# A hybrid attention layer: the running sums of the forget gates and the first layer of the compressed branch at other places in TensorE's queue

## The chip, the cores and the metric

The kernel runs on one core of a Trainium2 chip, in one launch. The metric is the device time of a run in microseconds. A core has a matrix engine (TensorE, PE in the profile; its loads of stationary operands are PEld), a vector engine (VectorE, DVE), a scalar engine for activation functions (ScalarE, ACT), a general engine (GpSimd, POOL) and an engine that mostly starts transfers (SyncE, SP). Each works through a queue of its own in order and waits on semaphores for what the others have made. SBUF holds the tiles, PSUM the results of matmuls, HBM the weights.

## The reference, cut to what matters

Two layers on a sequence of 512 rows of 1024 numbers. Each layer is a feed-forward block, a block of token mixing and another feed-forward block, with a layer norm behind each. The token mixing projects the rows with one wide matrix into the queries, keys and values of three kinds of attention and some gates:

```
q_a, kv_a, g_a, q_b, k_b, v_b, q_c, k_c, v_c, f_c = _split_cols(h @ w_in)
o_a = _nsa(q_a, kv_a, g_a, ...)          # compressed + selected + window
o_b = _swa_sink(q_b, k_b, v_b, sinks, ...)  # window of 128, with a sink
o_c = _fox(q_c, k_c, v_c, f_c, b_f)      # forget gates
```

Two pieces of it are touched here. The forget gates enter as a running sum over the sequence:

```
log_f = jax.nn.log_sigmoid((f_c + b_f).astype(jnp.float32))
c = jnp.cumsum(log_f, axis=1)
logits = q @ k * scale + c[query] - c[key]
```

And the compressed branch of the first kind makes one key and one value out of each 32 rows, with a small two-layer network, `gelu(flat @ w1) @ w2`, where `flat` has 2048 numbers and the hidden layer has 256.

## The kernel before

All numbers are four bytes wide. Where a product has to be exact, an operand is split into a high and a low part, and three matmuls (high by high, low by high, high by low; L161, L162 and L163 in `mm3`) add up in PSUM. One slice `k` of a projection is thus three matmuls of 128 x 128 by 512 columns, and a projection of 128 output columns is eight such slices, called parts here.

The function `mix` is the token mixing. TensorE's and GpSimd's instructions run in exactly the order in which the code issues them (a manual schedule). Those of VectorE, ScalarE and SyncE are ordered by the tile framework, which also puts in the semaphores and hands out the buffers of a pool; tiles that share a tag share its buffers.

The order of TensorE's work is made by two things. A double-ended queue `fill` holds closures: `chunk` (L826) appends the eight parts of a projection, and the last part calls the evacuation of the result from PSUM. `pump(n)` (L891) pops and runs closures until n of them have counted; those wrapped by `free` (L809) don't count. A function `step` (L970) works on batches of attention units, `cur` and `prev`. It issues the scores of `cur` (`u.s()`) and the transposes of the probabilities of `prev` (`u.tr()`) in turn, with parts from `fill` between them, and ends with the value products of `prev` (`u.pv`, into the PSUM tile `po`). Ahead of a unit's scores it pumps until `need(u)` holds, that is, until its query and keys have been made. The list `PUMPS` (L1010) says how many closures go into each of the 21 steps. The first eight batches are pairs of units of the windowed attention (`Swa`), the later ones are units of the forget-gate attention (`Fox`) and of the first kind (`Nsa`).

The names that matter:

- `ev_q` (L398) takes a query from PSUM into the tile `qs`: a ScalarE copy (L403) and a VectorE subtraction (L404), twice, one behind the other. `set_q` (L841) lets it count as made four places further down in `fill`.
- `ev_gf` (L438) takes the gates from PSUM; its `rest` transposes them on TensorE (`gfT`, L445) and runs a chain of small VectorE and ScalarE instructions up to the logarithm of the forget gates (`f`, L465). Its `cum` (L471) makes the running sums with seven small matmuls a layer against a triangle of ones or ones alone (`cum`, L475 and L478; each matmul of this kind is two records, so 28 in two layers), and the result goes through HBM (`ncd`) to tiles `nck`. `set_gf` (L899) puts `late`, which calls `rest`, at place 4 of `fill` and `cum` at place 14 or the end.
- `ev_z` (L489) takes the compressed key's or value's projection from PSUM and adds position codes: eight VectorE additions (L500, L502) into two tiles `z`, which take buffers of the tag `p`. This tag has 14 buffers (`PB`) and mostly holds probabilities.
- `conv` (L506) is the first layer of the compressed branch. Before, it is eight closures `part(j)`. Each takes a buffer of the tag `raw` (three buffers, shared with all weights that stream in), loads two transfers of 256 KB into it and issues four matmuls with a 128 x 64 stationary operand and 256 columns (`hid`, L522, eight records). Keys go to rows 0 to 63 of the result and values to rows 64 to 127. Behind the last one comes the gelu. `tr` transposes the result (`glT`), and `conv2` (L547) is the second layer.
- `ps` hands out PSUM buffers by tag: two of `mm` for projections, three of `sc` for scores and for `hid`, two of `tp` for transposes, one of `po` for value products.

Before, the stage issues 29 closures ahead of the first step: the windowed attention's key, its first query, the gates, half of its second query and the gate transposes. The running sums follow behind the second half of that query. The compressed key, the third query and the compressed value come next, and then the eight parts of `conv` one by one between parts of the fourth query and the first `Fox` projections.

Of the kernel before, what the change touches and what calls it, by code (L numbers as in the profile page):

```python
# [9 lines left out]
F32 = mybir.dt.float32  # L10
# [8 lines left out]
P = 128  # L19
# [45 lines left out]
def body(tc, a, out, depth=DEPTH):  # L65
    nc = tc.nc
# [46 lines left out]
    def wraw(shape=None):  # L113
        return wt.tile(list(shape or [P, KD, P]), F32, name="raw", tag="raw", bufs=3)
# [237 lines left out]
    def mix(l, wts, pend, done_ffn, xap, xa, nxt):  # L352
        m = K()
        PB = 14
# [151 lines left out]
        def conv(ws):  # L506


            c = K()
            wv = [w.rearrange("(c p) f -> p c f", p=P) for w in ws]  # L510

            def part(j):
                def go():
                    if j == 0:
                        c.p = ps("sc", "hid", (P, 256))
                    r = wraw([P, 2, 2, 256])
                    for i in range(2):
                        nc.sync.dma_start(r[:, i], wv[i][:, 2 * j:2 * j + 2])
                    for k in (2 * j, 2 * j + 1):
                        for i in range(2):  # L520
                            z = (m.zk, m.zv)[i][k // 8][:, k % 8].rearrange("p g n -> p (g n)")
                            nc.tensor.matmul(c.p[64 * i:64 * i + 64], z, r[:, i, k % 2], start=k == 0, stop=k == 15)  # L522
                    if j == 7:
                        x = at.tile([P, 2, 256], F32, name="gl", tag="p", bufs=PB)
                        t, c.t = x[:, 0], x[:, 1]
                        nc.scalar.activation(t, c.p, AF.Square)
                        nc.vector.tensor_scalar(t, t, 0.044715, 1.0, op0=OP.mult, op1=OP.add)
                        nc.vector.tensor_tensor(t, t, c.p, op=OP.mult)
                        nc.scalar.activation(t, t, AF.Tanh, scale=GELU_C)
                        nc.vector.scalar_tensor_tensor(c.t, t, 1.0, c.p, op0=OP.add, op1=OP.mult)  # L530
                return go

            def tr():
                pt = ps("tp", "glT", (P, 2, P))
                for f in range(2):
                    nc.tensor.transpose(pt[:, f], c.t[:, f * P:(f + 1) * P], ident)
                x = at.tile([P, 3, P], F32, name="glt", tag="p", bufs=PB)
                c.gk = x[:, 0].rearrange("p (f n) -> p f n", f=2)
                c.gv = x[:, 1:3].rearrange("p f (g r n) -> p f g r n", g=2, r=2)
                nc.vector.tensor_copy(c.gk, pt[:, :, 0:64])  # L540
                for f in range(2):
                    nc.vector.tensor_copy(c.gv[:, f], pt[:, f, 64:P].rearrange("p (g n) -> p g n", g=2)[:, :, None]
                                          .to_broadcast([P, 2, 2, NSLOT]))

            return c, [part(j) for j in range(8)], tr

        def conv2(c):  # L547

# [255 lines left out]


        fill = deque()
        FREE = "free"

        def free(f):  # L809
# [16 lines left out]
        def chunk(c0, then, w=w_in, load=wcols):  # L826
            st = K()

            def part(i):
                def go():  # L830
                    if i == 0:
                        st.w = load(w, c0)
                        st.p = ps("mm", "pj")
                    proj(st.p, st.w, ks=range(i, i + 1))
                    if i == 7:
                        then(st.p)
                return go

            fill.extend(part(i) for i in range(8))

        def set_q(lst, i):  # L841
            def go(p):
                t = ev_q(p)
                fill.insert(min(4, len(fill)), free(lambda: lst.__setitem__(i, t)))
            return go
# [45 lines left out]
        def pump(n=1):  # L891
            while n > 0 and fill:
                n -= fill.popleft()() is not FREE

# [4 lines left out]
        def set_gf(p):  # L899
            rest = ev_gf(p)  # L900

            def late():
                m.cum = rest()
            fill.insert(min(4, len(fill)), late)
            fill.insert(min(14, len(fill)), lambda: m.cum())


        chunk(CKB, set_kb)
        chunk(CQB, set_q(m.qb, 0))
        chunk(0, set_gf, load=lambda w, c0: wgf())  # L910
        chunk(CQB + P, set_q(m.qb, 1))
        pump(29)
        chunk(CKV + 0, lambda p: setattr(m, "zk", ev_z(p, 0)))
        chunk(CQB + 2 * P, set_q(m.qb, 2))
        chunk(CKV + P, lambda p: setattr(m, "zv", ev_z(p, 1)))
        cv, parts, tr = conv([a["cmp_k_w1"][l], a["cmp_v_w1"][l]])
        n0 = len(fill)
        chunk(CQB + 3 * P, set_q(m.qb, 3))
        fox_chunks(0)
        rest = [fill.pop() for _ in range(len(fill) - n0)][::-1]  # L920
        for i, f in enumerate(rest):
            fill.append(f)
            if i >= 6 and parts:
                fill.append(parts.pop(0))
        fill.append(tr)
        chunk(CKV + 2 * P, nsa_k(0))
        fill.append(lambda: conv2(cv))
        chunk(CKV + 4 * P, nsa_k(1))
        chunk(CQA, set_q(m.qa, 0))
        fox_chunks(1)  # L930
        chunk(CQA + P, set_q(m.qa, 1))
        fox_chunks(2)
# [37 lines left out]
        def step(cur, prev, n):  # L970


            for u in cur:
                while not need(u):
                    pump(1)
                    n -= 1
            it, iu = chain(u.tr() for u in prev), chain(u.s() for u in cur)
            nt, ns = sum(u.ngrp for u in prev), sum(u.nseg for u in cur)
            slots = max(nt, ns, 1)
            done = 0  # L980

            def upto(x):
                nonlocal done
                x = int(round(x))
                if x > done:
                    pump(x - done)
                    done = x

            last = min(2, max(n, 0))
            n -= last  # L990
            for j in range(slots):
                if j * ns // slots != (j + 1) * ns // slots or slots == ns:
                    next(iu, None)
                upto(n * (2 * j + 1) / (2 * slots))
                if j * nt // slots != (j + 1) * nt // slots or slots == nt:
                    next(it, None)
                upto(n * (j + 1) / slots)
            for _ in iu:
                pass
            for _ in it:  # L1000
                pass
            pump(last)
            if prev:
                po = ps("po", "po", (P, 4, P))
                for j, u in enumerate(prev):
                    u.pv(po[:, j])
                for j, u in enumerate(prev):
                    nc.scalar.activation(o_t[u.br][u.m][:, u.qb * P:(u.qb + 1) * P], po[:, j], AF.Copy)

# [201 lines left out]
```

## Time and profile before

| what | value |
|---|---|
| median of three runs | 2587.15 us (2585.22 to 2590.07) |
| the profiled execution | 2589.08 us |
| its span in the profile | 2587.4 us |
| mean granted TensorE clock | 0.996 of full |
| TensorE busy | 2558.4 us, 13099 matmuls |
| VectorE, ScalarE busy | 1212.7 us, 960.9 us |
| records of `hid`, both layers | 128, 18.6 us busy |

The profile is one execution. A row of the timeline has the start and length in microseconds from the start of the span, the engine, the line of the kernel, the operation, output and input by the names of their tiles, the shape, and how many instructions are merged into it; in brackets stand the idle time before it and what ended it. Matmuls overlap, so a row's length is more than its share of the queue; the distance of two starts is the better measure. A row of waits has the waiting instruction, what it waited for, the total in microseconds, the number of times and the longest.

### The profile page before, as it was taken

The page shows a single profiled execution, that of the slowest core. Times are in us where ns is not written, and L with a number is a line of the kernel's source. Part 1 is how long each engine was busy: PE and PEld are TensorE (multiplying, and loading weights), DVE is VectorE, ACT ScalarE, POOL GpSimd, SP SyncE. Part 2 cuts the span into 40 slices and gives each one's busy share as a digit, 9 for nine tenths or more (in the row PEclk, how much of TensorE's full clock was granted, in tenths as well). Part 3 has the DMA queues.
Part 4 walks back from the last instruction along what each step waited for, and adds up shares of the span by engine and source line. Part 5 has one row for each costly group of instructions (what it writes and reads, how often), then busy time and mean ns, then how long its engine had stood idle before and what let it go on. Part 6 is the DMA issues. An engine that isn't in the chain of part 4 may idle for free.

```text
span 2587.4 us, 34084 instructions
## 1 busy us (share of the span) xinstructions
PE 2558.4 (99%) x13099; PEld 2110.0 (82%) x13099; DVE 1212.7 (47%) x2633; ACT 960.9 (37%) x2015; POOL 210.9 (8%) x419
## 2 busy tenths in 40 slices
PE   9999999999999999999999999999999999999998
PEld 8888887788888888888888888877888888888887
DVE  4444244677654354442344432556766434533323
ACT  3222223577733232222232221345777323322211
POOL 0000000244300000000000000002432000000000
PEclk9999999999999999999999999999999999999999
DMA  6333333421143433333333332424221534233331
GB/s 214 110 96 98 98 92 102 138 73 52 46 140 89 125 107 96 95 96 96 114 90 95 96 96 97 127 71 138 62 59 34 151 98 142 83 98 98 98 91 64
DMA packets 360835, 256.39 MB, mean 99 GB/s; under 512 B 15336, under 2 KB 341032, under 8 KB 360672
## 3 DMA queue, kind: packets, MB, share of 16 engines
q1 hardware_dynamic: 359520, 250.02, 32.7%
q0 software_dynamic: 1152, 4.19, 0.4%
q8 instruction: 103, 1.69, 0.3%
q14 instruction: 60, 0.49, 0.1%
HBM read 247.83 MB, written 9.49 MB: 99 GB/s over the span
## 4 chain that ended last, share of the span: by engine, by line
PE 93%; DVE 4%; ACT 2%; issue 1%; DMA 0%; POOL 0%; POOLq 0%; DVEq 0%; ACTq 0%
PE acc L176 7%; PE acc L174 7%; PE acc L175 7%; PE pg L161 6%; PE pg L163 6%; PE pg L162 6%; PE pu L163 6%; PE pu L162 6%; PE pu L161 6%; PE pj L161 4%; PE pj L163 4%; PE pj L162 4%; PE gate L161 3%; PE gate L163 3%; PE gate L162 3%; PE brp L161 2%
## 5 line engine op out<-in xcount | busy, mean ns | idle before, releaser
L141 DVE TENSOR_TENSOR lo<-raw,hi 128x1024 fp32r<-128x1024 f32 (+2 forms) x470 | 500.9, 1074 | 853.5 <-ACT hi L140 852.3
L140 ACT ACTIVATE hi<-raw 128x1024 fp32r<-128x1024 f32 (+2 forms) x470 | 430.6, 930 | 1224.7 <-issue 707.3
L161 PE MATMUL pj<-xh,hi 128*128 128x512 f32 (+1 forms) x704 | 265.1, 377 | 0.8 <-DVE qs L404 0.7
L161 PE MATMUL pg<-xh,hi 128*128 128x512 f32 x640 | 249.9, 390 | 0.0
L163 PE MATMUL pj<-xh,lo 128*128 128x512 f32 (+1 forms) x704 | 249.4, 354 | 0.3 <-DVE lo L141 0.3
L162 PE MATMUL pj<-xl,hi 128*128 128x512 f32 (+1 forms) x704 | 248.7, 353 | 0.9 <-DVE xl L221 0.9
L162 PE MATMUL pg<-xl,hi 128*128 128x512 f32 x640 | 249.5, 390 | 0.0
L163 PE MATMUL pg<-xh,lo 128*128 128x512 f32 x640 | 249.5, 390 | 0.0
L163 PE MATMUL pu<-xh,lo 128*128 128x512 f32 x640 | 249.0, 389 | 0.0
L161 PE MATMUL pu<-xh,hi 128*128 128x512 f32 x640 | 249.0, 389 | 0.0
L162 PE MATMUL pu<-xl,hi 128*128 128x512 f32 x640 | 249.0, 389 | 0.0
L174 PE MATMUL acc<-hi,ha 128*128 128x512 f32 x576 | 227.3, 395 | 0.0
L175 PE MATMUL acc<-hi,ha 128*128 128x512 f32 x576 | 227.3, 395 | 0.0
L176 PE MATMUL acc<-lo,ha 128*128 128x512 f32 x576 | 227.2, 395 | 0.0
L203 POOL TENSOR_SCALAR st<-st 128x1 f32<-128x1 f32 x24 | 6.3, 264 | 1903.1 <-ACT junk L201 1903.1
L286 DVE TENSOR_TENSOR t<-t,pu 128x512 f32<-128x512 f32 x80 | 55.0, 687 | 216.6 <-PE pu L163 216.6
L161 PEld LDWEIGHTS pj<-xh,hi 128*128 128x128 f32 x704 | 134.0, 190 | 21.3 <-issue 7.2
L163 PEld LDWEIGHTS pj<-xh,lo 128*128 128x128 f32 x704 | 133.0, 189 | 19.8 <-DVE lo L141 0.5
L162 PEld LDWEIGHTS pj<-xl,hi 128*128 128x128 f32 x704 | 133.8, 190 | 11.5 <-DVE xl L221 1.6
L162 PEld LDWEIGHTS pg<-xl,hi 128*128 128x128 f32 x640 | 120.6, 188 | 25.1
L161 PEld LDWEIGHTS pg<-xh,hi 128*128 128x128 f32 x640 | 120.5, 188 | 25.1
L163 PEld LDWEIGHTS pg<-xh,lo 128*128 128x128 f32 x640 | 120.5, 188 | 25.0
(243 smaller groups left out, 4417.6 us busy)
## 6 DMA issues: line engine op xcount, KB each, us to landing
raw<-in_ffn_w_dram SPq DMA_DIRECT2D x264, 512.0 KB, 3.8
raw<-in_w_in_dram SPq DMA_DIRECT2D x56, 512.0 KB, 4.1
raw<-in_w_gate_dram SPq DMA_DIRECT2D x48, 512.0 KB, 4.0
raw<-in_w_out_dram SPq DMA_DIRECT2D x16, 512.0 KB, 3.5
x_sp<-xa POOLq DMA_DIRECT2D x8, 512.0 KB, 6.6
tab<-bvec SPq DMA_DIRECT2D x16, 256.0 KB, 2.8
raw<-in_cmp_k_w_dram SPq DMA_DIRECT2D x16, 256.0 KB, 2.7
raw<-in_cmp_v_w_dram SPq DMA_DIRECT2D x16, 256.0 KB, 3.3
```

The costliest lines, as they stand in the source:

```text
L140: nc.scalar.activation(hi[:, c], raw[:, c], AF.Copy)
L141: nc.vector.tensor_tensor(lo[:, c], raw[:, c], hi[:, c].bitcast(F32), op=OP.subtract)
L161: nc.tensor.matmul(o, hi[:, k], vh, start=first, stop=False)
L162: nc.tensor.matmul(o, hi[:, k], vl, start=False, stop=False)
L163: nc.tensor.matmul(o, lo[:, k], vh, start=False, stop=last)
L174: nc.tensor.matmul(o, sh(k)[:, t], hi[:, c], start=k == 0, stop=False)
L175: nc.tensor.matmul(o, sl(k)[:, t], hi[:, c], start=False, stop=False)
L176: nc.tensor.matmul(o, sh(k)[:, t], lo[:, c], start=False, stop=k == nk - 1)
L203: nc.gpsimd.tensor_scalar(st[:, 4:5], st[:, 3:4], 1.0 / D, EPS / ALPHA ** 2, op0=OP.mult, op1=OP.add)
L286: nc.vector.tensor_tensor(t, t, pu, op=OP.mult)
```

## The change

It does five things, all in the token mixing.

1. The gates' transposes and chain start right behind the gates' projection and the first scores, since only 24 closures are pumped ahead of the steps. The compressed key and value are projected next, one behind the other, then the second and third query. The running sums are a closure behind the third query.
2. `conv` gives a function `feed` in place of the list of parts. A call of it, if fewer than four are waiting, takes a buffer of the tag `p`, starts the two transfers (of 128 KB each) for one slice `k` of the first layer's weights, and appends the slice's two matmuls to a queue `narrow`. Calls of `feed` are put between the parts of the third and fourth query and the first `Fox` projections, and don't count.
3. `step` empties `narrow` right behind the value products of `prev`, before the ScalarE copies.
4. `end` (in place of `tr`) issues what is left and then the transposes. It stands behind the projections of the two keys of the first kind, and `conv2` goes in two parts from the end of the projection after them.
5. Where `prev` has two groups of transposes, both are issued at one place, the second, and no longer at two.

```
-            def part(j):
+            def load(k):
+                r = at.tile([P, 2, 256], F32, name="cw1", tag="p", bufs=PB)
+                for i in range(2):
+                    nc.sync.dma_start(r[:, i], wv[i][:, k])
+
                 def go():
-                    if j == 0:
+                    if k == 0:
                         c.p = ps("sc", "hid", (P, 256))
-                    r = wraw([P, 2, 2, 256])
                     for i in range(2):
-                        nc.sync.dma_start(r[:, i], wv[i][:, 2 * j:2 * j + 2])
-                    for k in (2 * j, 2 * j + 1):
-                        for i in range(2):
-                            z = (m.zk, m.zv)[i][k // 8][:, k % 8].rearrange("p g n -> p (g n)")
-                            nc.tensor.matmul(c.p[64 * i:64 * i + 64], z, r[:, i, k % 2], start=k == 0, stop=k == 15)
-                    if j == 7:
+                        z = (m.zk, m.zv)[i][k // 8][:, k % 8].rearrange("p g n -> p (g n)")
+                        nc.tensor.matmul(c.p[64 * i:64 * i + 64], z, r[:, i], start=k == 0, stop=k == 15)
+                    if k == 15:
...
-            return c, [part(j) for j in range(8)], tr
+            c.n = 0
+
+            def feed():
+                if c.n < 16 and len(narrow) < 4:
+                    narrow.append(load(c.n))
+                    c.n += 1
+
+            def end():
+                while narrow or c.n < 16:
+                    feed()
+                    narrow.popleft()()
+                tr()
+
+            return c, feed, end
...
-            fill.insert(min(14, len(fill)), lambda: m.cum())
...
         chunk(0, set_gf, load=lambda w, c0: wgf())
+        pump(24)
+        chunk(CKV + 0, lambda p: setattr(m, "zk", ev_z(p, 0)))
+        chunk(CKV + P, lambda p: setattr(m, "zv", ev_z(p, 1)))
         chunk(CQB + P, set_q(m.qb, 1))
-        pump(29)
-        chunk(CKV + 0, lambda p: setattr(m, "zk", ev_z(p, 0)))
+        cv, feed, tr = conv([a["cmp_k_w1"][l], a["cmp_v_w1"][l]])
+        n0 = len(fill)
         chunk(CQB + 2 * P, set_q(m.qb, 2))
-        chunk(CKV + P, lambda p: setattr(m, "zv", ev_z(p, 1)))
-        cv, parts, tr = conv([a["cmp_k_w1"][l], a["cmp_v_w1"][l]])
-        n0 = len(fill)
+        fill.append(lambda: m.cum())
         chunk(CQB + 3 * P, set_q(m.qb, 3))
         fox_chunks(0)
         rest = [fill.pop() for _ in range(len(fill) - n0)][::-1]
         for i, f in enumerate(rest):
+            fill.append(free(feed))
+            if i % 2:
+                fill.append(free(feed))
             fill.append(f)
-            if i >= 6 and parts:
-                fill.append(parts.pop(0))
+        chunk(CKV + 2 * P, nsa_k(0))
+        chunk(CKV + 4 * P, nsa_k(1))
         fill.append(tr)
-        chunk(CKV + 2 * P, nsa_k(0))
-        fill.append(lambda: conv2(cv))
-        chunk(CKV + 4 * P, nsa_k(1))
         chunk(CQA, set_q(m.qa, 0))
+        fill.insert(len(fill) - 2, lambda: conv2(cv))
...
+            pair = 2 if nt == 2 else 1
+            nt //= pair
...
-                    next(it, None)
+                    for _ in range(pair):
+                        next(it, None)
...
                 for j, u in enumerate(prev):
                     u.pv(po[:, j])
+                while narrow:
+                    narrow.popleft()()
```

More of the change, by code (lines that the diff above doesn't have):

```diff
@@ L806, in mix @@
         fill = deque()
+        narrow = deque()
         FREE = "free"
```

## The prediction

> **What bounds the kernel now.** I read the page first: its busy times and the chain that ended last.
>
> ```profile
> span 2587.4 us, 34084 instructions
> PE 2558.4 (99%) x13099; PEld 2110.0 (82%) x13099; DVE 1212.7 (47%) x2633; ACT 960.9 (37%) x2015; POOL 210.9 (8%) x419
> ...
> PE 93%; DVE 4%; ACT 2%; issue 1%; DMA 0%; POOL 0%; POOLq 0%; DVEq 0%; ACTq 0%
> ```
>
> TensorE is the bound: busy for 99% of the span and 93% of the chain. An edit gains only where it removes time from TensorE's own queue: a wait, slow matmuls, or a switch between kinds of matmul. So next I read TensorE's waits in the first layer's mixing stage, and the windows around its longest.
>
> ```profile
> PE cum L475 <- DVE f L465: 3.6, 1, 3.6
> ...
> PE pj L161 <- DVE qs L404: 0.3, 1, 0.3
> ```
>
> ```profile
> 437.00:442.00 5.00, 5.00 (x18) 3.12 (x17) 1.40 (x5) 0.00 (x0) 0.57 (x1) 0.60 0.03 7
> 1717.00:1721.00 4.00, 3.61 (x12) 1.58 (x13) 1.62 (x7) 1.76 (x6) 0.57 (x1) 0.57 0.43 130
> ```
>
> The largest wait is that of the running sums for the forget gates' vector chain, 3.6 us. The windows (length, busy PE, PEld, DVE, ACT and POOL, granted clock, DMA share, GB/s) show that behind it the clock falls to 0.60 in layer 1 and 0.57 in layer 2. The timeline of TensorE tells what that costs.
>
> ```profile
> 430.89 0.64 PE L607 MATMUL sS<-ks,qs 128*128 128x256 f32 x4
> 435.13 0.59 PE L475 MATMUL cum<-tri,f 128*8 128x128 f32 x2 [3.60 <-DVE f L465]
> 435.51 1.48 PE L478 MATMUL cum<-ones,f 128*8 128x384 f32 x2
> ...
> 438.92 0.63 PE L475 MATMUL cum<-tri,f 128*8 128x128 f32 x2
> 439.48 0.80 PE L161 MATMUL pj<-xh,hi 128*128 128x512 f32 x1
> ...
> 440.93 0.44 PE L161 MATMUL pj<-xh,hi 128*128 128x512 f32 x1
> ```
>
> ```profile
> 1713.15 0.64 PE L607 MATMUL sS<-ks,qs 128*128 128x256 f32 x4
> 1717.39 0.42 PE L475 MATMUL cum<-tri,f 128*8 128x128 f32 x2 [3.60 <-DVE f L465]
> 1717.61 1.49 PE L478 MATMUL cum<-ones,f 128*8 128x384 f32 x2
> ...
> 1721.33 0.50 PE L161 MATMUL pj<-xh,hi 128*128 128x512 f32 x1
> ```
>
> **The change, part by part.** *Running sums.* A projection record is 0.39 us long and the next one starts 0.23 later (419.63 to 419.85 below), so a record outlasts its slot by 0.16, and the four sS records of 0.64 hold the queue for 0.48. Layer 1: the queue is free at 430.89 + 0.48 = 431.37, and the next projection matmul starts at 439.48: 8.1 us. The three matmuls from 439.48 to 440.93 took 1.45 us; at 0.23 each they take 0.69: 0.76 more. Layer 2: 1713.63 to 1721.33, 7.7 us. In their new place the sums come after 32 more projection parts of 3 × 0.23 = 0.69 us, 22 us behind the gate transposes where it was four parts and one set of scores, so the chain is done and I expect no wait. They still cost their own time: 435.13 to 439.48 is 4.35 us at about half clock, so about 2.2 at full (the first pair of layer 2, 1717.39 to 1717.61, did take 0.22 where the last of layer 1, 438.92 to 439.48, took 0.56), and I add 0.2 for going in and out. **Gain: 8.9 − 2.4 = 6.5 and 7.7 − 2.4 = 5.3, together 11.8 us.** If half of the chain's wait returned, 3.6 of it would be lost.
>
> *First layer of the compressed branch.* Now eight runs of eight records stand alone between full-width matmuls.
>
> ```profile
> 467.78 0.40 PE L163 MATMUL pj<-xh,lo 128*128 128x512 f32 x1
> 468.11 1.86 PE L522 MATMUL hid<-raw,z 128*64 128x256 f32 x8
> 469.90 0.73 PE L607 MATMUL sS<-ks,qs 128*128 128x256 f32 x4
> ...
> 475.19 0.39 PE L163 MATMUL pj<-xh,lo 128*128 128x512 f32 x1
> 475.51 1.08 PE L522 MATMUL hid<-raw,z 128*64 128x256 f32 x8
> 476.52 0.50 PE L161 MATMUL pj<-xh,hi 128*128 128x512 f32 x1
> 476.86 0.40 PE L162 MATMUL pj<-xl,hi 128*128 128x512 f32 x1
> ```
>
> The eight starts of a run lie (1.08 − 0.38) / 7 = 0.10 apart, so its work is 0.80 us. But from the free slot at 475.19 + 0.23 = 475.42 to the next projection at 476.52, and 0.11 lost behind it (0.34 to the following start for 0.23), a run takes 1.21: 0.41 us goes into changing to 64-wide matmuls and back. The first run takes 0.78 more (1.86 for 1.08), waiting for the additions that make z. In the new order four runs of sixteen follow value products, which are 64-wide too and pay for the change already. **Gain per layer: 8 × 0.41 + 0.78 = 4.06, both layers 8.1 us.** That a value product is followed by these without a change is nowhere in the trace; bounds: four changes of 0.41 per layer kept (gain 4.8 in all), or none (8.1). I take none: they have the same shape of output. The weights come in 32 transfers of half the size per layer for 16 of this kind (size and median time to landing):
>
> ```profile
> raw<-in_cmp_v_w_dram SPq DMA_DIRECT2D x16, 256.0 KB, 3.3
> ```
>
> Each is asked for at least five projection parts (3.5 us) ahead of its matmul, and SyncE's queue is not on TensorE's path, so I cost this at nothing; without that cover it is one landing, some 3 us a layer. The probability ring (14) holds four z, four weights and at most four probabilities.
>
> *The new order's own wait.* The second query projection moves from ahead of the sums to behind both compressed projections, and scores need it soon: counting the queue's parts, the scores of its first block are issued two parts (6 × 0.23 = 1.39 us) after its last matmul. Before, a whole step lay between. What an evacuation of a query takes is shown by the first one.
>
> ```profile
> 419.63 0.39 PE L162 MATMUL pj<-xl,hi 128*128 128x512 f32 x1
> 419.85 0.39 PE L163 MATMUL pj<-xh,lo 128*128 128x512 f32 x1
> ...
> 421.28 0.59 ACT L403 ACTIVATE qs<-pj 64x512 fp32r<-64x512 f32 x1
> ...
> 422.09 0.68 DVE L404 SCALAR_TENSOR_TENSOR qs<-pj,qs 64x512 fp32r<-64x512 f32 x1
> ...
> 422.81 0.59 ACT L403 ACTIVATE qs<-pj 64x512 fp32r<-64x512 f32 x1 [0.94 <-DVE qs L404]
> ...
> 423.44 0.69 DVE L404 SCALAR_TENSOR_TENSOR qs<-pj,qs 64x512 fp32r<-64x512 f32 x1 [0.66 <-ACT qs L403]
> ```
>
> From the last projection matmul (419.85) to the end of the fourth link (424.13) are 4.28 us. Two parts cover 0.23 + 1.39 = 1.62, and a start follows its releaser by 0.14: a wait of 2.8 us. While VectorE is crowded it is more; the third query projection shows that:
>
> ```profile
> 453.37 0.39 PE L163 MATMUL pj<-xh,lo 128*128 128x512 f32 x1
> ...
> 458.71 0.69 DVE L404 SCALAR_TENSOR_TENSOR qs<-pj,qs 64x512 fp32r<-64x512 f32 x1
> ```
>
> Here 6.03 us, so a wait of 4.5. It is crowded at the new place, since both z now follow each other:
>
> ```profile
> L502 DVE TENSOR_TENSOR z<-vt,peT x16: 562/578/589, 448.4 to 1746.5; 64x248 f32<-64x248 f32 x16
> L500 DVE TENSOR_TENSOR z<-vt,peT x16: 576/581/595, 452.1 to 1749.4; 64x256 f32<-64x256 f32 x16
> ```
>
> Sixteen additions of 0.58 a layer are 9.3 us in some 14 us of TensorE time. But nothing new arrives for VectorE while TensorE waits. I take 3.0 us, nearest to the first row: **loss 2 × 3.0 = 6.0 us**, bounds 0 (only the first half of the query is needed for the first scores) and 4.5 a layer. Behind the waiting scores stand all projections, so nothing hides it.
>
> The row of layer 2 (3.6 us of idle, then clock 0.57) says that such a wait can cost more than itself. The Trainium skill, "TensorE: Matmul & The Clock Gate", section "HAM oscillation — how this bites in real kernels", asks for no idle gap over about 3.4 us. By that rule a wait of 3.0 costs only itself and the sum stays; one of 4.5 would run what follows at half clock. The trace has only gaps of 3.6, which agree.
>
> *End of the stage.* The eight old parts counted as fillers, and 29 parts were issued ahead of the steps; now it is 24. So before, two filler parts were left for the last step, and now there are none.
>
> ```profile
> 1986.45 0.66 PE L683 MATMUL ptF<-ident,p 128*128 128x128 f32 x4
> ...
> 1988.76 1.03 PE L783 MATMUL ptN<-ident,p 128*128 128x128 f32 x8
> 1990.29 0.30 PE L789 MATMUL ptC<-ident,pc 128*128 128x128 f32 x1 [0.49 <-DVE p L393]
> ...
> 1992.12 1.09 PE L690 MATMUL po<-p,v 128*64 128x128 f32 x16
> ```
>
> From the first transposes to the value products are 5.67 us with two fillers (1.39) among them. Seven groups share two buffers, so evacuation sets the pace; without fillers up to three parts (2.05 us) of cover are gone. I take 1.2 a layer: **loss 2.4 us**, bounds 0 and 4.1. The steps with four units in their turn get up to three parts more between their transposes; I count nothing.
>
> *Paired transposes.* Four transposes in a row cost what twice two do (0.11 each), so no gain; the first unit's evacuation now ends nearer to the value products, with 2.8 us of parts between. I take 0.2 a layer: **0.4 us**, bounds 0 and 2.
>
> **Sum:** −11.8 − 8.1 + 6.0 + 2.4 + 0.4 = −11.1 us. The profiled execution took 2589.08 (span 2587.4 and 1.7 around it), so 2578.0; it lay 1.9 above the median of the three runs, 2587.15, which becomes **2576.0 us**.
>
> **The rivals.** *The query wait is hidden* (both halves early, no loss at the end): −11.8 − 8.1 + 2 = 2569. For it: TensorE has no other wait like this in the list; against it: the four links of 4.28 us. *The wait trips the clock*: 4.5 us and about 2 more at half clock (layer 2: 3.5 us at 0.57 loses near 1.7), 6.5 a layer: −19.9 + 13 + 2.8 = 2583. For it: the crowded 6.03 us and both gaps of 3.6 that did so. *It doesn't do what it says*: switches remain inside the runs, or weights land late, 3.3 us a layer: 2583. *Slower: VectorE becomes the bound* between the first scores and the second query.
>
> ```profile
> 425.00:470.00 45.00, 41.26 (x214) 30.65 (x212) 30.05 (x101) 19.54 (x58) 4.46 (x10) 0.92 0.22 67
> ```
>
> It has 30 us of work in 45 us there. In the new order some 26 of it (both z 9.3, the splits, the gate chain, four units) come in the first 22, ahead of the second query: a backlog of 4 us, behind which all four links could stand (4.5), and the clock loss of two windows, 3: 11.5 a layer, −19.9 + 23 + 2.8 = +5.9, 2593. It decides from 8.6 us of wait a layer. Against it: the z additions and splits are ready well ahead, and VectorE needn't take them all first.
>
> **How the numbers follow.** Forecast 0.46 (2576, alone 2572 to 2580); hidden wait 0.20 (2569); clock tripped 0.17 (2583); not what it says 0.08 (2583); slower 0.09 (2593). The range reaches from the hidden wait with the bounds of the smaller terms, 2566, to the tripped clock with the loss at the end in full, 2588. A measurement tells about 0.2%, 5.2 us, from no change: under 2582 is faster. Forecast and hidden wait are (0.66), and of the two at 2583 somewhat under half (0.10): 0.76. The rest of those, 0.15, is within; slower 0.09.
>
> **What would show it.** The sums' row without a wait, and first pairs 0.22 apart; no window of the stage under 1.00 in clock; rows of hid x16 right behind po, at 0.10 a start; a wait of sS for qs near 3 us once a layer; more waits among the last transposes. It is wrong if the list of waits has one of over 4 us a layer, or if hid keeps gaps of 0.2 to po.

## The result and the profile after

The changed kernel takes **2593.17 us** (median of 20 runs, 2589.06 to 2594.89) where the kernel before took 2587.36 (20 runs beside it): a ratio of 1.0022, 95% interval 1.0015 to 1.0029. It is slower by 5.7 us, where 11.1 us less were forecast; the range ended at 2588.

The page of the changed kernel, first the span, then the busy times of the engines:

```profile
span 2591.0 us, 34195 instructions
...
PE 2554.0 (99%) x13099; PEld 2113.3 (82%) x13099; DVE 1215.4 (47%) x2631; ACT 961.5 (37%) x2017; POOL 205.2 (8%) x419
```

The same 13099 matmuls, TensorE still busy for 99%, and yet 3.6 us more span with 4.4 us less busy time: waits have come in. The list of TensorE's waits in layer 1's mixing stage names them (what waited, for what, total in us, times, longest):

```profile
PE sS L621 <- DVE qs L404: 2.1, 2, 1.2
PE ptC L803 <- ACT p L395: 1.9, 1, 1.9
PE po L655 <- ACT p L395: 1.5, 1, 1.5
PE ptN L797 <- POOL p L602: 1.2, 2, 1.0
PE ptS L647 <- ACT vbd L585: 1.1, 1, 1.1
PE kv L574 <- DMA cw2k<-in_cmp_k_w_dram: 0.9, 1, 0.9
PE ptF L697 <- ACT p L395: 0.9, 2, 0.7
```

In layer 2 the first of these is larger:

```profile
PE sS L621 <- DVE qs L404: 2.9, 2, 2.0
```

The sums' 3.6 us are gone from the list. In their place stand waits that the kernel before did not have or had smaller. The timeline of TensorE shows the first three places:

```profile
442.01 1.14 PE L655 MATMUL po<-p,v 128*64 128x128 f32 x12 [1.51 <-ACT p L395]
443.08 0.72 PE L161 MATMUL pj<-xh,hi 128*128 128x512 f32 x1
...
449.58 0.44 PE L621 MATMUL sS<-ks,qs 128*128 128x128 f32 x2 [1.19 <-DVE qs L404]
450.93 0.44 PE L621 MATMUL sS<-ks,qs 128*128 128x128 f32 x2 [0.91 <-DVE qs L404]
```

```profile
456.85 1.09 PE L655 MATMUL po<-p,v 128*64 128x128 f32 x16
457.77 1.90 PE L522 MATMUL hid<-cw,z 128*64 128x256 f32 x16
459.60 0.74 PE L621 MATMUL sS<-ks,qs 128*128 128x256 f32 x4
```

The last three rows are what the change is for: sixteen products of the first layer directly behind the value products, 1.83 us from start to start, without a gap. That part works. But behind the wait at 442.01 a projection matmul takes 0.72 us for 0.39. The windows view (length, busy PE, PEld, DVE, ACT, POOL, granted clock, DMA share, GB/s) says why:

```profile
443.20:446.60 3.40, 3.40 (x9) 2.63 (x10) 3.31 (x6) 0.44 (x2) 0.00 (x0) 0.50 0.10 33
...
709.40:712.90 3.50, 3.50 (x26) 3.17 (x27) 0.69 (x1) 0.60 (x1) 0.00 (x0) 0.51 0.02 5
```

```profile
1733.40:1736.90 3.50, 3.09 (x8) 2.58 (x9) 1.19 (x7) 0.97 (x5) 0.00 (x0) 0.51 0.87 245
1859.70:1863.20 3.50, 3.50 (x13) 2.85 (x12) 3.04 (x17) 3.33 (x13) 2.00 (x6) 0.51 0.47 137
```

Four times in the two stages the granted clock halves for 3.4 us, which costs some 1.7 us each; in the kernel before it was one stretch of 6.8 us and one of 3.4. Each of the four stands at one of the new waits: 443.2 behind that of po, 709.4 among three short ones of the last step (0.99, 0.24 and 0.38 us), 1733.4 at those of sS and 1859.7 behind that of ptC.

To see where the time sits, I cut each layer's stage at its value products. Step n ends with the n-th run of `po`; 20 of them make a layer. A step's loss is its length less the slots of its matmuls (0.23 us for a projection matmul, 0.11 for a transpose, 0.05 for a value product, and so on); the slots add up to 273.4 us a layer in every kernel here. Losses of both layers together, in us, from the profiled executions:

| steps | before | after | late sums alone (first experiment) | six weight tiles (last experiment) |
|---|---|---|---|---|
| 1 | 15.5 | 6.0 | 3.7 | 2.4 |
| 2 | 1.4 | 10.5 | 1.4 | 1.3 |
| 3 to 6 | 14.0 | 6.5 | 12.5 | 7.2 |
| 7, 8 | 3.1 | 9.4 | 3.1 | 8.2 |
| 9 to 19 | 24.2 | 27.6 | 24.5 | 23.3 |
| 20 | 3.5 | 7.6 | 3.5 | 3.5 |
| length of both stages | 608.5 | 614.6 | 595.5 | 592.6 |

The change gains 17 us in the steps it is aimed at (1 and 3 to 6) and loses 23 in all the others.

### The profile page after: what moved, and what is told of

Same layout as the page of the kernel before. It is cut to its first block, busy times and chain, and to the rows that moved or that the text cites. A ratio compares the mean times of both kernels' runs of the same rounds, so it can differ in the third digit from the quotient of the medians.

```text
span 2591.0 us, 34195 instructions
## 1 busy us (share of the span) xinstructions
PE 2554.0 (99%) x13099; PEld 2113.3 (82%) x13099; DVE 1215.4 (47%) x2631; ACT 961.5 (37%) x2017; POOL 205.2 (8%) x419
## 4 chain that ended last, share of the span: by engine, by line
PE 94%; DVE 2%; ACT 1%; DMA 1%; issue 1%; POOL 0%; SPq 0%; POOLq 0%; DVEq 0%; ACTq 0%
PE acc L174 7%; PE acc L175 7%; PE acc L176 7%; PE pg L161 6%; PE pg L162 6%; PE pg L163 6%; PE pu L162 6%; PE pu L163 6%; PE pu L161 6%; PE pj L161 5%; PE pj L162 4%; PE pj L163 4%; PE gate L161 3%; PE gate L163 3%; PE gate L162 3%; PE brp L163 2%
```

## The experiments

**Theories.** The first: the gains came as forecast, and new waits, each with its own cause, ate them. The rivals: (1) VectorE is full in this stretch, so that a wait which goes is only moved; (2) the pairing of transposes is the main cause; (3) the half-clock windows cost the time, not the waits; (4) all of it comes from the order of the projections and the second query's wait. Each time is a median, and each ratio is to the kernel before on the same chip, with its interval; "us" behind a ratio is that ratio times 2587.

### Late sums alone

On the kernel before:

```
-            fill.insert(min(14, len(fill)), lambda: m.cum())
...
         chunk(CQB + 2 * P, set_q(m.qb, 2))
+        fill.append(lambda: m.cum())
```

> The kernel before with one part of the change alone: the running sums are issued behind the third query's chunk; chunk order, first layer of the compressed branch and transposes stay as before. In the kernel before the sums' wait and the half-clock window beside it stand in the first step of each layer (loss 8.29 and 7.19 us); with the change that step lost 3.02 us in both layers. Theory (the forecast gains came, new waits elsewhere ate them): faster than before by about 8 to 12 us, near 2577, because none of the new waits belongs to this part. Rival 1 (VectorE is full in this stretch, so a wait that goes is only moved): within 2 us of before, about 2586, with a wait on VectorE or ScalarE work in the first two steps in place of the old one. Rival 2 (pairing of transposes is the cause of the loss): same as the theory here, 8 to 12 us faster.

2573.97 us, 0.9952 [0.9940, 0.9965], **12.4 us faster than before**. The forecast's 11.8 stands. The timeline shows the sums without a wait, their pairs 0.22 us apart, and the first run of the compressed branch:

```profile
443.87 0.39 PE L475 MATMUL cum<-tri,f 128*8 128x128 f32 x2
444.09 0.81 PE L478 MATMUL cum<-ones,f 128*8 128x384 f32 x2
...
461.46 1.08 PE L522 MATMUL hid<-raw,z 128*64 128x256 f32 x8
```

That first run had taken 1.86 us before (from 468.11), waiting for VectorE's last additions for z, which ended at 468.84; here they end at 460.60, ahead of the run, and it takes 1.08 without having been touched. So the rest of the change, everything but the sums, costs some 18 us.

### Sums early again in the changed kernel

```
         chunk(CKV + 0, lambda p: setattr(m, "zk", ev_z(p, 0)))
+        fill.insert(min(8, len(fill)), lambda: m.cum())
...
-        fill.append(lambda: m.cum())
```

> The changed kernel with one part undone: the running sums are issued early again, eight projection steps behind the forget gates' transposes, everything else as changed. Theory: the sums are worth what the forecast said also within the changed kernel, so it is slower than the changed kernel by 6 to 12 us, near 2601. Rival 1 (a wait that goes is only moved: the changed kernel pays in the second query's wait what it saved on the sums): within 2 us of the changed kernel, about 2593. A faster time would say that the later place itself does harm.

2593.46 us, 1.0033 [1.0023, 1.0043]: 2.8 us above the changed kernel, and the intervals overlap, and the runs of this kernel spread over 7.8 us (2591.1 to 2598.9). The theory's 6 to 12 is wrong. The time comes close to that of rival 1, but no wait has been moved: the waits of the changed kernel are all there, and that of the sums comes on top. The wait is back, but smaller (waits of TensorE, layer 1):

```profile
PE sS L621 <- DVE qs L404: 2.1, 2, 1.2
PE cum L475 <- DVE f L465: 2.0, 1, 2.0
...
PE po L655 <- ACT p L395: 1.4, 1, 1.4
```

From the gate transposes to the end of the chain are 7.8 us as in the kernel before (420.66 to 428.49 here, 427.21 to 434.98 there). But seven projection parts instead of four stand between the transposes and the sums now, so the sums wait 2.0 instead of 3.6. And in layer 2 of this profile no half-clock window fell on step 2 (it lost 3.42 instead of 5.57). A gain measured alone is not the same gain in another order.

### Without pairing

```
-            pair = 2 if nt == 2 else 1
+            pair = 1
```

> The changed kernel with the pairing of transposes undone: each of the two small transposes groups of a step has its own place again, the rest as changed. In the changed kernel three waits could come from pairing: po on ScalarE's copy of p in the first step (1.51 us a layer, followed by a half-clock window in layer 1), ptS on ScalarE's vbd in the seventh (1.11), po on VectorE's p in the eighth (0.39). Theory (pairing is a small part: it gains 0.41 us for each run of another tile size that it saves and costs these waits): 1 to 6 us faster than the changed kernel, 2587 to 2592, ptS gone and po smaller. Rival 2 (pairing is the main cause): 8 us or more faster than the changed kernel, at or below 2585. Rival 1: po's wait stays as it is, since VectorE's backlog of additions for the compressed keys sets it, and the time stays within 1.5 us of the changed kernel's.

2592.11 us, 1.0026 [1.0016, 1.0036]: no difference from the changed kernel. ptS's wait goes and another takes its place (waits, layer 1):

```profile
PE po L655 <- ACT p L395: 2.4, 2, 1.8
...
PE kv L574 <- DVE stS L597: 1.2, 1, 1.2
```

Rival 2 falls. The time is the one that rival 1 gave, and po's wait in step 1 is no smaller (1.8 us for 1.5).

### Second query ahead of the compressed projections

```
         pump(24)
+        chunk(CQB + P, set_q(m.qb, 1))
         chunk(CKV + 0, lambda p: setattr(m, "zk", ev_z(p, 0)))
         chunk(CKV + P, lambda p: setattr(m, "zv", ev_z(p, 1)))
-        chunk(CQB + P, set_q(m.qb, 1))
```

> The changed kernel with the second query's chunk ahead of both compressed chunks, as it stood before the change; the rest as changed. In the changed kernel the second query's scores (sS) wait for VectorE's qs 1.19 + 0.91 us in layer 1 and 2.01 + 0.91 in layer 2, and half-clock windows of 3.41 us stand beside. Theory: sS waits gone, the step behind them loses about 0.7 us again as in the kernel before instead of 4.97 and 5.57, so 6 to 9 us faster than the changed kernel, about 2585. Rival 1 (VectorE full): the wait appears again at po or at the first layer's weights in the same stretch, and less than 3 us are gained. Rival 3 (the clock is what costs, not the waits): half-clock windows stay in these steps although the waits are gone, and the gain is below the waits' own 5 us.

2583.09 us, 0.9994 [0.9985, 1.0003]: about 7 us below the changed kernel by the ratios, as the theory had it. The wait for qs is gone, and step 1 loses 1.18 us for 3.02. But in step 2 a new one stands, and VectorE's rows say what it is:

```profile
451.26 0.66 PE L655 MATMUL po<-p,v 128*64 128x128 f32 x8
454.37 1.07 PE L655 MATMUL po<-p,v 128*64 128x128 f32 x8 [2.45 <-DVE p L393]
455.22 3.21 PE L522 MATMUL hid<-cw,z 128*64 128x256 f32 x16
```

```profile
448.61 0.59 DVE L500 TENSOR_TENSOR z<-vt,peT 64x256 f32<-64x256 f32 x1
...
452.36 0.56 DVE L502 TENSOR_TENSOR z<-vt,peT 64x248 f32<-64x248 f32 x1
...
453.62 0.69 DVE L393 COPY p<-ptS 128x512 f32<-128x512 f32 x1
```

Eight additions for the compressed keys, 448.61 to 452.9, stand ahead of the copy of the transposed probabilities, which TensorE had made by 448.60. The copy starts at 453.62, behind them, so the value products wait for additions that they have nothing to do with. Here rival 1 is right in part: some of the query's wait had been moved.

### The two compressed projections apart

```
         chunk(CKV + 0, lambda p: setattr(m, "zk", ev_z(p, 0)))
-        chunk(CKV + P, lambda p: setattr(m, "zv", ev_z(p, 1)))
         chunk(CQB + P, set_q(m.qb, 1))
+        chunk(CKV + P, lambda p: setattr(m, "zv", ev_z(p, 1)))
```

> The changed kernel with only the second compressed chunk moved behind the second query's chunk: first compressed, second query, second compressed, third query. The two compressed chunks, each with eight additions on VectorE (0.56 to 0.59 us each), are then not adjacent, and the second query's chunk stands halfway between its place before and its place after. Theory: the wait of the query's scores for qs goes (chunk issued eight steps sooner), the first value products wait no longer for the copy behind the additions, so the first two steps lose some 2 to 4 us a layer instead of 8: 2582 to 2587, like the query's chunk first (2583.1). Rival 1 (VectorE full, total work counts and not its order): within 3 us of the changed kernel, 2590 or more.

2588.14 us, 1.0001 [0.9993, 1.0010], 5.4 us less than the changed kernel, just outside what the theory gave. sS waits 0.32 us a layer for 2.1 and 2.9; po's 1.51 in step 1 stays, since the first eight additions still come right there.

### The order before, with late sums and the moved first layer

```
         pump(24)
+        chunk(CQB + P, set_q(m.qb, 1))
         chunk(CKV + 0, lambda p: setattr(m, "zk", ev_z(p, 0)))
+        chunk(CQB + 2 * P, set_q(m.qb, 2))
         chunk(CKV + P, lambda p: setattr(m, "zv", ev_z(p, 1)))
-        chunk(CQB + P, set_q(m.qb, 1))
...
-        chunk(CQB + 2 * P, set_q(m.qb, 2))
```

> The changed kernel with the chunk order of the kernel before in full (second query, first compressed, third query, second compressed chunk), sums late and first layer inside the value products as changed: the late sums alone (2574.0 us) plus the first layer's move and the pairing. Theory (many small waits): the first two steps lose no more than in the run with late sums alone (1.85 and 0.69 us a layer), the first layer's steps gain 2.7 us a layer, but the waits of the seventh to fifteenth and of the twentieth step stay (some 5 us a layer): 2574 to 2581, no faster than the late sums alone. Rival 4 (the whole loss comes from the order of these chunks and the wait of the second query): 2565 to 2570, faster than the late sums alone by the forecast's 8 less its 2.4 for the end. Rival 1 (VectorE full): the wait shows again at po in the first two steps, 2580 to 2586.

2591.61 us, 1.0014 [1.0005, 1.0023]; every theory gave less. Steps 1 and 2 are clean (1.18 and 0.70), so the order is what makes their waits: with the second query ahead of both sets of additions and the third between them nothing waits there (with the second alone between them, po's 1.51 us had stayed). But now the first layer starts a step later, and step 6 lost 5.25 and 3.70 us, glT waiting 2.54: `end` is reached while products are still left, takes them in one piece, and stands before an activation that has just begun. Steps 7 to 20 lose as much as in the changed kernel or more. Rival 4 falls: the order is only one part.

### Three projection parts kept for the end, on that order

```
-        PUMPS = [11] * 8 + [10, 10, 12] * 4 + [8]
+        PUMPS = [11] * 5 + [10] * 3 + [10, 10, 12] * 4 + [8]
```

> The kernel with the old chunk order, late sums and moved first layer, with three projection steps fewer in three early steps, so that some are left to stand between the transposes of the last step, where the changed kernel had none and lost 2.99 to 4.60 us a layer against 1.73 before. Theory: the last step loses 1.7 us or less again and its half-clock windows go: 2.5 to 5 us faster than the same kernel without this edit. Rival: the last step's wait is on the normalisation by GpSimd and comes out the same with other work in between, or the steps that gave up their projection steps lose as much: within 1.5 us.

2581.90 us, 0.9978 [0.9969, 0.9987], **9 us faster** for one line, twice what was expected. Steps 9 to 19 go from 28.9 to 23.6 us of loss, step 20 from 9.1 to 3.5. What is left is in step 6:

```profile
497.89 3.14 PE L522 MATMUL hid<-cw,z 128*64 128x256 f32 x16 [0.89 <-DMA cw<-in_cmp_k_w_dram]
...
503.63 0.41 PE L536 MATMUL glT<-ident,gl 128*128 128x128 f32 x2 [2.60 <-DVE gl L530]
```

### The same line in the changed kernel

```
-        PUMPS = [11] * 8 + [10, 10, 12] * 4 + [8]
+        PUMPS = [11] * 5 + [10] * 3 + [10, 10, 12] * 4 + [8]
```

> The changed kernel, its chunk order included, with one edit: three early steps take ten projection steps instead of eleven, so that the steps after them stand where they stood before the change. The same edit on the old chunk order took 2591.6 us to 2581.9 and turned steps 11, 12, 15 and 20 back to their losses of before the change. Theory (the change took the first layer out of the list of projection steps without taking it out of the plan of how many a step takes, so the list runs three ahead and out before the last step): 7 to 11 us faster than the changed kernel, 2582 to 2586, with the waits ptC <- ScalarE's p (1.9 us) and ptN <- GpSimd's p (0.99) in these steps gone, and the first two steps unchanged at 8 us of loss. Rival (the old order is needed for that too, as those waits come from which chunk's evacuation falls into the step): under 3 us.

2583.68 us, 0.9988 [0.9979, 0.9997]: **8.8 us faster than the changed kernel**, steps 1 and 2 untouched. TensorE's waits from step 11 on in layer 1, first of the changed kernel, then of this one:

```profile
PE ptC L803 <- ACT p L395: 1.9, 1, 1.9
PE ptN L797 <- POOL p L602: 1.2, 2, 1.0
PE ptF L697 <- ACT p L395: 0.9, 2, 0.7
PE ptN L797 <- DVE pc L393: 0.4, 1, 0.4
```

```profile
PE ptC L803 <- ACT p L395: 0.6, 1, 0.6
PE ptN L797 <- ACT p L395: 0.6, 1, 0.6
PE ptC L803 <- DVE p L393: 0.5, 1, 0.5
PE ptN L797 <- DVE pc L393: 0.3, 1, 0.3
PE ptN L797 <- POOL p L602: 0.3, 1, 0.3
```

The second list is that of the kernel before, to 0.1 us:

```profile
PE ptN L783 <- ACT p L395: 0.7, 1, 0.7
PE ptC L789 <- ACT p L395: 0.6, 1, 0.6
PE ptC L789 <- DVE p L393: 0.5, 1, 0.5
PE ptN L783 <- DVE pc L393: 0.3, 1, 0.3
PE ptN L783 <- POOL p L588: 0.3, 1, 0.3
```

The change took eight parts out of `fill` and pumped five fewer ahead, so the list ran three parts early through the whole stage. Every evacuation of a projection met other attention work than before, and the last step had no part to stand between its transposes.

### Second query first, and three parts kept

Both edits on the changed kernel:

```
         pump(24)
+        chunk(CQB + P, set_q(m.qb, 1))
...
-        chunk(CQB + P, set_q(m.qb, 1))
...
-        PUMPS = [11] * 8 + [10, 10, 12] * 4 + [8]
+        PUMPS = [11] * 5 + [10] * 3 + [10, 10, 12] * 4 + [8]
```

> The changed kernel with both edits: second query's chunk ahead of the compressed chunks, and three projection steps less in the early steps. Theory: the two gains, about 10 us of the first and about 9 of the second, add, as they stand in different steps: 2572 to 2577, level with the late sums alone (2574.0); what is left are po's wait in the second step (2.45 us a layer) and the seventh step's kv and ptS. Rival 3 (half-clock windows wander to other gaps and take the gain back): 2578 to 2584.

2578.07 us, 0.9963 [0.9950, 0.9977], 15 us below the changed kernel where 7.2 and 8.8 make 16: the two add, nearly. The time is 1 us above the theory's range, at the lower end of rival 3's. The profile does show a half-clock window in step 2 of both layers, at po's wait of 2.48 us, but the profiled execution was the slowest of the five (2583.25 us; the others took 2576.8 to 2578.4), so how many windows the others had isn't shown.

### Second layer's weights earlier; the first layer's end later

Two attempts on the kernel of the old order with three parts kept. The first asks for `cw2k` and `cw2v` with the last of the first layer's weights:

```
                     c.n += 1
+                    if c.n == 16:
+                        c.w2 = load2()
```

> As the kernel before it in this list (old order, late sums, moved first layer, projection steps left for the last step), with the second layer's weights of the compressed branch issued when the last of the first layer's weights is, instead of at the products that use them. In the changed kernel they wait 0.91 us a layer on SyncE's queue, which stood 10.89 us at a projection weight's load until its buffer came free. Theory: kv's wait goes, but the two tile buffers that the pair of transposes wants behind it (1.11 us) stay, so 1 to 2 us faster than without this edit. Rival: kv then waits for something else at the same time, under 0.7 us.

2582.64 us, 0.9983 [0.9974, 0.9991]: nothing gained; the rival was right. In the kernel without this edit kv already waits for ScalarE (0.63 us) and not for the weights, and with it that wait is 0.64. The second:

```
-        fill.append(tr)
         chunk(CQA, set_q(m.qa, 0))
-        fill.insert(len(fill) - 2, lambda: conv2(cv))
+        fill.insert(len(fill) - 4, tr)
+        fill.append(lambda: conv2(cv))
```

> Old chunk order, late sums, moved first layer, three projection steps kept for the end, and the first layer's end with its transposes four projection steps later, the second layer's products two later. In the same kernel without this edit the sixth step lost 6.44 and 4.65 us, since the end takes the last eight products and then waits 2.60 us for VectorE's activation of them (glT). Theory: glT's wait shrinks by what four projection steps last (4 x 0.68 us), 2 to 5 us faster than without this edit, 2577 to 2580. Rival: the end still runs in one piece, the products and the wait for the activation directly behind each other, so glT's wait is unchanged and the time too (2582).

2583.37 us, 0.9985 [0.9976, 0.9994]: the rival was right. `end` still runs in one piece; glT waits 2.32 us, in step 7 now, and the products ahead of it wait 1.76 and 1.88 us for their weights.

### Six weight tiles at a time

On the kernel of the old order with three parts kept:

```
-                if c.n < 16 and len(narrow) < 4:
+                if c.n < 16 and len(narrow) < 6:
```

> As the kernel without the later transposes (old order, late sums, three projection steps kept for the end), but up to six of the first layer's sixteen weight tiles are held at a time instead of four, so that runs of 6, 6 and 4 pairs of products behind the value products finish one step earlier, before the list reaches their end. Theory: the first layer's last products no longer wait for their weights (0.89 us in layer 1), the activation has a step's time, glT's wait of 2.60 us and the half-clock window behind it go, 6 to 9 us faster: 2573 to 2576. If the sixth step is then as in the kernel with the second query first (0.98 us of loss), and the second layer's products wait as before, it could beat the late sums alone (2574.0). Rival (six tiles of the probability ring are missing elsewhere): new waits for p in the first steps, no gain.

**2571.34 us, 0.9940 [0.9928, 0.9953]: 15.5 us faster than before, and the lowest median of all** (its interval overlaps that of the late sums alone). It is 9.8 us below the kernel without the edit, where 6 to 9 were expected. The products run in 6, 6 and 4 pairs and are done a step before `end`. Step 6 loses 0.66 us. The mean granted clock of both stages is 1.00 (columns as above), and the list of waits in layer 1 begins with:

```profile
407.00:703.00 296.00, 291.41 (x2020) 238.07 (x2020) 205.60 (x813) 195.48 (x636) 94.56 (x176) 1.00 0.27 77
1681.00:1977.00 296.00, 291.02 (x2016) 237.64 (x2016) 205.63 (x813) 195.42 (x636) 93.93 (x176) 1.00 0.27 77
```

```profile
PE po L655 <- ACT p L395: 1.4, 2, 1.2
PE kv L574 <- ACT p L395: 0.9, 1, 0.9
```

Its five runs spread over 1.1 us, the twenty of the changed kernel over 5.8.

This settles rivals 1 and 3 too. VectorE is busy for 411.2 us of both stages here and for 412.8 in the changed kernel (`after`, 408 to 715 and 1692 to 1999), so it wasn't its load that held TensorE up in steps 1 and 2 but what stood in front of what. And the half-clock windows of the changed kernel cost some 4 x 1.7 = 6.8 us, those of the kernel before some 5.1 (half of 6.8 + 3.4): 1.7 of the 3.6 us between the two spans.

## Why the prediction was wrong

The measured +5.7 us miss the forecast's -11.1 by 16.8. Three kernels stand between before and after, and the ratios give the price of each part on this path:

| part | from, to | forecast | measured |
|---|---|---|---|
| running sums | before, late sums alone | -11.8 | -12.4 |
| first layer and pairing | late sums alone, six weight tiles | -8.1 + 0.4 | -3.1 |
| order of the projections (and four tiles for six) | six weight tiles, changed kernel with three parts kept | +6.0 | +12.4 |
| end of the stage | changed kernel with three parts kept, after | +2.4 | +8.8 |
| sum | | -11.1 | +5.7 |

By the intervals each measured part is uncertain by some 3 us; the lengths of the stages in the four profiles, worked out in the same way, give -13.0, -2.9, +12.9 and +9.1.

The second and third row depend on the path. By the kernel of the old order with three parts kept, which has the changed kernel's four weight tiles, the first layer and pairing cost +6.7 (0.9952 to 0.9978) and the order +2.6 (0.9978 to 0.9988), because with four tiles the old order pays 6.44 and 4.65 us in step 6. Six tiles in the new order were not run. On either path the two rows together are +9.3, where -1.7 was forecast. By place, the changed kernel with three parts kept loses some 12 us more than the late sums alone in steps 1 and 2 and some 5 more in steps 7 and 8, and some 7 less in steps 3 to 6. The paragraphs below go by place.

**Running sums: right**, in mechanism and size: step 1 loses 11.8 us less (15.5 to 3.7), and the rest of the 12.4 is the first run of the compressed branch.

**First layer: mechanism right, size off.** The runs behind the value products do save the change of matmul kind: steps 3 to 6 lose 5.3 us less in both layers together (12.5 to 7.2) where 8 x 0.41 a layer had given 6.6. The 0.78 us a layer for the first run's wait was counted here but belongs to the sums' wait; it went with the sums alone. And 5.1 us come back in steps 7 and 8 (3.1 to 8.2), where the second layer now stands: kv waits 0.9 and po 1.2 us a layer for ScalarE's copies. The forecast had costed the move of `conv2` at nothing.

**The new order's own wait: half the price missing.** The scores' wait for the query was forecast at 3.0 us a layer and is 2.1 and 2.9. What failed is the step that priced this wait alone. The eight additions for the first z (432.5 to 436.8) stand ahead of VectorE's work on the scores (L597), which the exponentials need, and so hold up ScalarE's copy of the first transposes. VectorE's and ScalarE's rows in the changed kernel:

```profile
436.26 0.57 DVE L502 TENSOR_TENSOR z<-vt,peT 64x248 f32<-64x248 f32 x1
436.85 0.42 DVE L597 CUSTOM_DVE_ANT_0 p<-sS,tab 128x256 f32<-128x256 f32 x1
...
438.42 0.51 ACT L634 ACTIVATE p<-p,stS 128x256 f32<-128x256 f32 x1 [1.52 <-DVE stS L630]
...
441.59 0.85 ACT L395 ACTIVATE p<-ptS 128x256 f32<-128x256 f32 x2
```

The copy at 441.59 stands behind four exponentials, the first of which waited for VectorE until 438.42, a projection's evacuation and the split of a weight; that is po's 1.51 us a layer. And the windows at half clock, which the forecast allowed only from 4.5 us, came behind waits of 1.5 to 2 us. Two of the four stand here (443.2 and 1733.4), 1.7 us each. The waits of both layers (5.0 for sS, 3.0 for po) and these two windows make 11.4 us. The forecast had argued that "nothing new arrives for VectorE while TensorE waits"; but what VectorE already had stood in front of what TensorE needed.

**End of the stage: the step that failed most in proportion** (8.8 us for 2.4). The forecast saw that three parts of cover were gone and priced the last step at 1.2 us a layer; that step lost 4.1 us more in both layers together, with a window. For the rest it said: "The steps with four units in their turn get up to three parts more between their transposes; I count nothing." That is where the other half went: ptC waits in step 11 and ptF in steps 12 and 15, ptC with a window behind it in layer 2. The one line of `PUMPS` shows that both come from the plan: with it these waits went, and on the old order too it was worth 9 us.

**The rivals.** The slower rival's time, 2593, is the measured one, but it isn't what happened: it asked for 11.5 us a layer between the first scores and the second query (8.6 to lose anything at all), and there are 3.6 and 4.4 of wait (po and sS), 5.3 and 6.1 with a window each. "The wait trips the clock" was true as a mechanism and too small as a sum. No rival named the displacement. Nor did either of the forecast's signs of being wrong appear: no wait comes to over 4 us a layer, and hid follows po without a gap. Both looked for one large failure; what came was many small waits.

What stays open: that the 5.7 us split exactly so. The parts are measured in this sequence, and the other path and the sums put back early (2.8 us, not 12) show that another sequence gives other parts. In which executions a window follows a wait wasn't controlled either.

## What to carry to other kernels

When filler work leaves a list that is dealt out by a fixed plan, deal out the plan anew: one line of it was worth 8.8 us here, more than the two waits of 3.6 us that the change was made to remove. When work is moved past other work, look for its helpers' rows on the other engines and for what they now stand in front of; eight additions ahead of one copy held up the value products for 2.45 us. And price a wait of 1.5 us or more with the half-clock window that may follow it, some 1.7 us each time.

## What the runs showed of the hardware

A wait far shorter than the 3.6 us of the kernel before can be followed by a window at half clock. The traces have twelve times the same wait in the same place, ptC's 1.9 us (two layers each of the changed kernel and five of the experiments, those without three parts kept): a window of 3.41 us began within 1.6 us behind six of them. Of waits between 2.0 and 2.6 us, 14 of 19 had one at or behind them; of the ten of 1.2 us ahead of po in step 8, with projections before and mostly projections after, none. The two kernels with no wait above 0.7 and 1.2 us (late sums alone, six weight tiles) have no window in their stages. The Trainium skill, "TensorE: Matmul & The Clock Gate", section "What's actually happening", describes a window of about 3.4 us that runs freely and doesn't start with the work; the lengths of 3.41 agree, and a free phase would explain that the same wait trips it in half the executions. The rule of the same page of the Trainium skill, section "HAM oscillation — how this bites in real kernels", no gap over about 3.4 us, is too generous here by the measurement. No run here separates the length of the wait from what surrounds it (most that tripped stand beside transposes or value products), so why some lengths trip and others don't stays open.
